# A two-layer hybrid backbone on one core: each engine's order set by a list scheduler in the kernel

## The chip, the cores and the metric

One Trainium2 chip, of which the program uses one core. A core has five engines that run at the same time, each through its own queue in order: TensorE (PE) multiplies matrices into PSUM, VectorE (DVE) and ScalarE (ACT) work on PSUM and SBUF, GpSimd (POOL) on SBUF, and SyncE (SP) issues most DMA transfers; GpSimd issues some too. They wait for each other by semaphores. The time is the device time of one execution, in microseconds (us); 1934.28 us is the median of three runs of the kernel before.

## The reference

Two layers over 512 latent tokens and 256 context tokens of 1024 channels, in float32. Each layer: a modulated norm, one input projection whose columns go to three head groups, an output projection with a gated residual, then a modulated norm, a SwiGLU feed-forward part and a gated residual:

```python
h_l = rmsnorm(x, norm1_g[i]) * (1.0 + sc1_l) + sh1_l
h_c = rmsnorm(ctx, norm1_g[i]) * (1.0 + sc1_c) + sh1_c
p_l = h_l @ w_in[i]
p_c = h_c @ w_in[i]
...
att_l = diff_attention(q_l, k_all, v_all, lam, subln_g[i], lam_init)
x = x + g1_l * mix_out(p_l, att_l, hy_params, sg_params, w_out[i])
x = x + g2_l * swiglu(rmsnorm(x, norm2_g[i]) * (1.0 + sc2_l) + sh2_l, ffn_w1[i], ffn_w2[i])
```

`mix_out` joins a Hyena group (two long convolutions, in the kernel by cosine and sine tables), a gMLP group (tokens mixed in chunks of 128) and differential attention (the difference of two softmaxes, with normalized and rotated queries and keys). The latent queries read context and latent keys, the context only itself; in the second layer the context is needed for its keys and values alone. The modulation values (shift, scale, gate) are a product of a conditioning vector with `ada_w`, six sections per layer.

## The kernel before

**Tiling.** Streams lie with channels on the partitions, eight tiles of 128 channels by 512 (latent) or 256 (context) tokens. Every operand of a large product is split into a high part (12 bits) and the exact rest, and `mm3` makes three multiplications of each pair: high by high (L251), high by low (L252), low by high (L253), 128x512 or 128x256 in size. A weight piece is fetched by SyncE into the arena FW, its high part is made by ScalarE (L232) and its low part by VectorE or GpSimd (L233) into the arena RW. R holds split operands, F float32 data, `banks` is PSUM (8 banks).

**Stages.** Four generators write the program: `lat_task` (the latent stream through both layers), `con_task` (the context stream), `side_task` (the filters' spectra, L902 and L903), `ada_task` (modulation, L401: 32 output columns a time, in four column groups of the array, eight instructions for a chunk of 256 channels; L375 turns the sums, L386 makes the gains G). `woven` takes the next step of whichever stream's matrix work is behind by hand-set rates (`CON`, `SIDE`, `ADA`, `WOVEN`). Memory is given out as the program is written: an arena's block or a PSUM bank goes to the next user when its owner's `free` has been called, so a later user waits for an earlier one on the chip.

**Order.** The instructions go to the framework in the order in which the generators write them. Its own scheduler then orders each engine's queue, by that order as priority and by its own durations, and adds the semaphores.

**Places that the prediction names.** `norm`: the squares are summed over channels (L279), a Newton iteration makes 1/rms (L261 to L267), TensorE spreads it over the partitions (L293), `modulate` scales and rounds on ScalarE (L503, L504), VectorE makes the low part (L507). `lambdas` and `rope_tables`: small constants, whose DMAs GpSimd issues and VectorE uses (L334, L354). `attend`: scores with 64 contracted rows, maximum (L683), factor (L686), exponentials on ScalarE (L688), the two softmaxes' difference (L692 to L694), transposes (L703), the product with the values. `sgu` is the gMLP group (L795 adds its bias). `fwd` of the Hyena group ends with rounding on ScalarE (L1036).

Of the kernel before, what the change touches and what calls it, by code (L numbers as in the profile page):

```python
# [9 lines left out]
F32 = mybir.dt.float32  # L10
# [6 lines left out]
P = 128  # L17
D = 1024
KT = D // P
SEQ = 512  # L20
# [18 lines left out]
class Buf:  # L39
    """A piece of an arena; emit-time lifetime, slices like a tile."""  # L40
# [11 lines left out]
class Arena:  # L52
    """Blocks of one tile, handed out longest-unused first, so that reuse waits little."""
# [40 lines left out]
    def fits(self, sizes):  # L94
        """Whether blocks of these units can be had, one beside the other."""
# [17 lines left out]
class Stream:  # L113
    """One token stream (latent or context) in channel-major form."""
# [10 lines left out]
# PSUM banks by use, arena sizes in KiB per partition.  # L125
BANKS = {"A": (0, 1, 6, 7), "S": (2, 3, 4, 5), "W": (6, 7), "P": (6, 7)}
UNITS = {"R": 104, "RW": 24, "F": 44, "FW": 24}
# Rates of the tasks in each phase (the latent stream has 10), and of the woven steps of each layer.
# [5 lines left out]
# Work of the latent and of the context stream that GpSimd does ("mix": 2 is all of it, 1 a half).  # L134
# [8 lines left out]
# Steps of the tasks that come first, the chunks of modulation weights that are fetched ahead, and  # L143
# the arenas of the weights of the first feed-forward tiles.
# [5 lines left out]
class Net:  # L150
# [16 lines left out]
    def woven(self, *tasks):  # L167
        """Generators (gen, rate) side by side; the matrix work of each grows at its rate.

        A rate may be a key of self.rates, which change with the phases."""  # L170
# [20 lines left out]
    def room(self, *sizes):  # L191
        """Waits until the float32 arena has room for the next step."""
        while not self.F.fits(sizes):
            yield "wait"

    def claim(self, n):
        """Waits until n units of the operand arena are spoken for by nobody."""
        while self.claimed + n > UNITS["R"]:
            yield "wait"
        self.claimed += n  # L200
# [22 lines left out]
    def tt(self, n, dtype=F32):  # L223
        """Tiny per-partition scratch, round robin."""
# [5 lines left out]
    def split(self, src, hi, lo, lo_eng=None):  # L230
        """hi = src rounded to 12 bits, lo = the rest, exactly."""
# [3 lines left out]
    def weights(self, src, *shape, pool=False, arena=None):  # L235
        """A split piece of weights of this shape; the low part by GpSimd if pool."""
# [8 lines left out]
    def mm3(self, out, terms):  # L245
        """out = sum of lhsT^T rhs over split terms: hi hi + hi lo + lo hi."""
# [9 lines left out]
    def rsqrt(self, ms, n, out=None):  # L256
        """1/sqrt by an exponent guess and three Newton steps."""
# [1362 lines left out]
```

## Time and profile before

| what | value |
|---|---|
| median of three runs | 1934.28 us (1927.73 to 1936.95) |
| span of the profiled execution | 1924.6 us |
| TensorE busy | 1813.6 us (94%) |
| VectorE busy | 1082.6 us (56%) |
| ScalarE busy | 689.1 us (36%) |
| GpSimd busy | 119.7 us (6%) |
| mean DMA rate | 128 GB/s |

The span runs from the first to the last instruction of one profiled execution; the timed runs are other executions, and their median lies 9.7 us above it. Matmuls are pipelined and a record's length contains the pipeline, so the pace of TensorE is read from start to start, not from the length of a record. The granted clock is the share of TensorE's full 2.4 GHz; 0.5 is its other level, 1.2 GHz, and a stretch between them is a mixture.

### The profile page before, as it was taken

To read this page: it belongs to the slowest core of one execution; us is meant where nothing else is said; L and a number is where in the kernel's file an instruction comes from. 1 tells how busy PE (TensorE), PEld (TensorE's weight loads), DVE (VectorE), ACT (ScalarE), POOL (GpSimd) and SP (SyncE) were. 2 spreads that over 40 slices of the span, in tenths; PEclk is the share of its full clock that TensorE was granted. 3 is DMA by queue.
4 is the path that set the end of the run, shared out by engine and by line. 5 is a ranking of instruction groups with operands and counts; after the bars stand their busy time and mean duration, and the time that the engine had idled before them with its cause. 6 is when DMAs were issued, how large, how long until landed. Compare 5 with 4: busy or idle time off the path is not lost.

```text
span 1924.6 us, 27933 instructions
## 1 busy us (share of the span) xinstructions
PE 1813.6 (94%) x11106; PEld 1558.6 (81%) x11106; DVE 1082.6 (56%) x2255; ACT 689.1 (36%) x1203; POOL 119.7 (6%) x128
## 2 busy tenths in 40 slices
PE   5799999789997999999999999899999999999999
PEld 2578898678776888888888888689988788888887
DVE  5677886778767523232423244789588773333333
ACT  2544434544544421212122112543455462222221
POOL 1100223211001000000000000011000000000000
PEclk9899899799997999999999999899999899999999
DMA  7567644235444343243424234444213222323231
GB/s 272 177 233 237 201 162 143 83 125 187 134 167 147 111 126 127 84 136 108 144 83 151 74 102 156 153 154 144 79 34 119 64 71 63 110 84 105 89 97 64
DMA packets 89564, 245.41 MB, mean 128 GB/s; under 512 B 9780, under 2 KB 21782, under 8 KB 89434
## 3 DMA queue, kind: packets, MB, share of 16 engines
q1 hardware_dynamic: 81162, 221.71, 35.2%
q0 software_dynamic: 8272, 21.92, 3.8%
q8 instruction: 87, 1.43, 0.3%
q14 instruction: 43, 0.35, 0.1%
HBM read 221.18 MB, written 22.41 MB: 127 GB/s over the span
## 4 chain that ended last, share of the span: by engine, by line
PE 79%; DVE 9%; DMA 4%; ACT 3%; issue 2%; POOL 0%; SPq 0%; ACTq 0%; DVEq 0%; POOLq 0%
PE banks L251 25%; PE banks L252 24%; PE banks L253 24%; PE banks L401 2%; PE banks L703 1%; DMA x_ctx<-F 1%; DVE RW L233 1%; DMA F<-x_ctx 1%; ACT F L688 1%; DVE tiny L683 1%; DVE F L1025 1%; PE banks L375 1%; PE banks L279 1%; DVE F L456 1%; DMA FW<-in_w_out 0%
## 5 line engine op out<-in xcount | busy, mean ns | idle before, releaser
L251 PE MATMUL banks<-R,RW 128*128 128x512 f32 (+1 forms) x1984 | 696.0, 352 | 9.1 <-ACT R L504 3.9
L252 PE MATMUL banks<-R,RW 128*128 128x512 f32 (+1 forms) x1984 | 693.9, 350 | 3.0 <-DVE R L507 3.0
L253 PE MATMUL banks<-R,RW 128*128 128x512 f32 (+1 forms) x1984 | 692.2, 349 | 0.5 <-DVE RW L233 0.5
L232 ACT ACTIVATE RW<-FW 128x1024 fp32r<-128x1024 f32 (+2 forms) x240 | 240.5, 1003 | 541.4 <-PE banks L252 418.9
L251 PEld LDWEIGHTS banks<-R,RW 128*128 128x128 f32 x1984 | 376.9, 190 | 64.7 <-ACT R L504 4.7
L252 PEld LDWEIGHTS banks<-R,RW 128*128 128x128 f32 x1984 | 377.0, 190 | 51.4 <-DVE R L507 3.8
L253 PEld LDWEIGHTS banks<-R,RW 128*128 128x128 f32 x1984 | 376.7, 190 | 50.4 <-issue 2.0
L233 DVE TENSOR_TENSOR RW<-FW,RW 128x1024 fp32r<-128x1024 f32 (+2 forms) x228 | 262.7, 1154 | 238.0 <-ACT RW L232 229.4
L1186 DVE SCALAR_TENSOR_TENSOR F<-banks,mods,F 128x512 f32<-128x512 f32 (+1 forms) x192 | 116.2, 615 | 177.4 <-PE banks L253 133.8
L251 PE MATMUL banks<-R 128*128 128x256 f32 (+3 forms) x584 | 188.0, 340 | 26.4 <-ACT R L1036 13.7
L252 PE MATMUL banks<-RW,R 128*128 128x256 f32 x624 | 180.0, 289 | 5.4 <-DVE RW L233 5.4
L251 PE MATMUL banks<-RW,R 128*128 128x256 f32 x624 | 181.1, 291 | 0.4 <-ACT F L552 0.2
L252 PE MATMUL banks<-R 128*128 128x256 f32 (+3 forms) x584 | 179.6, 319 | 1.4 <-DVE R L233 1.4
L253 PE MATMUL banks<-RW,R 128*128 128x256 f32 x624 | 180.2, 289 | 0.0
L253 PE MATMUL banks<-R 128*128 128x256 f32 (+3 forms) x584 | 177.5, 315 | 1.2 <-DVE R L1038 1.2
L251 PEld LDWEIGHTS banks<-R 128*128 128x128 f32 (+1 forms) x584 | 117.4, 209 | 49.6 <-ACT R L1036 15.2
L1204 DVE TENSOR_TENSOR F<-F,banks 128x256 f32<-128x256 f32 (+1 forms) x71 | 40.0, 565 | 208.5 <-PE banks L253 191.8
L232 ACT ACTIVATE R<-F 128x512 fp32r<-128x512 f32 (+1 forms) x133 | 72.0, 549 | 226.9 <-DVE F L1204 160.9
L252 PEld LDWEIGHTS banks<-R 128*128 128x128 f32 (+1 forms) x584 | 119.8, 209 | 10.0 <-issue 3.5
L252 PEld LDWEIGHTS banks<-RW,R 128*128 128x128 f32 x624 | 121.7, 195 | 7.6 <-DVE RW L233 6.3
L251 PEld LDWEIGHTS banks<-RW,R 128*128 128x128 f32 x624 | 121.5, 195 | 3.1 <-ACT F L552 0.8
L253 PEld LDWEIGHTS banks<-RW,R 128*128 128x128 f32 x624 | 121.8, 195 | 2.2 <-issue 1.5
(159 smaller groups left out, 1739.7 us busy)
## 6 DMA issues: line engine op xcount, KB each, us to landing
FW<-in_ffn_w SPq DMA_DIRECT2D x104, 512.0 KB, 3.7
FW<-in_ada_w SPq DMA_DIRECT2D x96, 512.0 KB, 5.0
FW<-in_w_in_tm SPq DMA_DIRECT2D x50, 512.0 KB, 4.8
R<-in_tab POOLq DMA_DIRECT2D x28, 512.0 KB, 4.9
FW<-in_w_in_cm SPq DMA_DIRECT2D x24, 512.0 KB, 4.7
F<-x_ctx SPq DMA_DIRECT2D x36, 256.0 KB, 3.6
FW<-in_ffn_w SPq DMA_DIRECT2D x24, 384.0 KB, 2.9
x_ctx<-F SPq DMA_DIRECT2D x32, 256.0 KB, 2.4
```

The costliest lines, as they stand in the source:

```text
L232: self.nc.scalar.activation(hi, src, AF.Copy)
L233: (lo_eng or self.nc.vector).tensor_tensor(lo, src, hi.bitcast(F32), op=ALU.subtract)
L251: mm(out, lhsT=lh, rhs=rh, start=(i == 0), stop=False)
L252: mm(out, lhsT=lh, rhs=rl, start=False, stop=False)
L253: mm(out, lhsT=ll, rhs=rh, start=False, stop=(i == n - 1))
L279: nc.tensor.matmul(p1[:, t:t + 1], lhsT=sq[:, t * P:(t + 1) * P], rhs=self.ones[:, 0:1], start=True, stop=True)
L375: nc.tensor.matmul(pt[:, b], lhsT=sb[:, b // 2, b % 2 * P:(b % 2 + 1) * P], rhs=self.pick, start=True, stop=True)
L401: nc.tensor.matmul(pa[32 * j:32 * j + 32, :], lhsT=self.cv[:, 4 * i + j, :], rhs=w[:, j, :], start=(i == 0), stop=(i == 1), tile_position= ...
L456: nc.vector.tensor_tensor(st.acc[:, cols], st.acc[:, cols], q.ap, op=ALU.add)
L683: nc.vector.tensor_reduce(m, b.ap, axis=AX.X, op=ALU.max)
L1186: self.nc.vector.scalar_tensor_tensor(x, p, self.mods[l][:, sec * 8 + k, st.v:st.v + 1], x, op0=ALU.mult, op1=ALU.add)
L1204: nc.vector.tensor_tensor(s.ap, s.ap, u, op=ALU.mult)
```

## The change

The generators, their rates and all arithmetic stay. What they call is no longer the framework but a recorder: `Plan.note` writes each instruction down with an engine, a duration (`took`), the time until its engine can take the next one (`pace`) and the pieces of memory that it writes and reads. At the end `needs` finds for each instruction those that it has to come after (values, and memory that is used again), `order` simulates the five engines and takes, whenever one is free, the ready instruction of the lowest rank, and `issue` hands the instructions to the framework in that order, with an edge from each to the next one on its engine, so that the framework's scheduler keeps it. The rank is three quarters the place in the old order and one quarter the length of the longest chain of work that hangs on the instruction. The rest of the diff deletes comments.

```diff
+class Plan:
...
+    def note(self, e, op, args, kw):
...
+        if op == "dma_start":
+            took, pace = math.prod(out.shape) * 4 / self.LINE, 50.0 if e == self.SP else 560.0
+        elif e == self.PE:
+            if op == "transpose":
+                pace, late, ins = 109.0, [args[1]], [args[2]]
+            else:
+                lhs, rhs = kw["lhsT"], kw["rhs"]
+                n, late, ins = size(rhs), [lhs], [rhs]
+                if rhs.dtype != F32 or lhs.dtype != F32:
+                    pace = max(n / self.RATE + 13.5, 109.0)
+                elif size(lhs) <= 32:
+                    pace = (2 * n / self.RATE + 6) / 4
+                else:
+                    pace = 2 * max(112.0, n / self.RATE)
+            took = pace + self.DRAIN
...
+    def order(self):
+        todo, needs = self.todo, self.needs()
+        n = len(todo)
+        rest, behind = [0.0] * n, [[] for _ in todo]
+        for k in range(n - 1, -1, -1):
+            rest[k] += todo[k][4] + (self.LANDING if todo[k][1] == "dma_start" else 0.0)
+            for j, kind in needs[k].items():
+                rest[j] = max(rest[j], rest[k])
+                behind[j].append((k, kind))
+        top = max(rest)
+        rank = [self.share * k / n - (1 - self.share) * rest[k] / top for k in range(n)]
...
+            now, e = best
+            while soon[e] and soon[e][0][0] <= now:
+                heapq.heappush(can[e], heapq.heappop(soon[e])[1:])
+            k = heapq.heappop(can[e])[1]
...
+    def issue(self):
+
+        nosync = mybir.DependencyInfo(mybir.DependencyClass.NoSync, mybir.DependencyReason.DATA)
+        last = [None] * 5
+        for k in self.order():
+            e, op, args, kw = self.todo[k][:4]
+            ins = getattr(getattr(self.tc.nc, Program.engines[e]), op)(*args, **kw).ins
+            if last[e] is not None:
+                self.tc.add_manual_dep(ins, last[e], nosync, reason="order")
+            last[e] = ins.name
+
+
 def network(ctx, tc, A):
+    tc = Plan(tc)
     net = Net(ctx, tc, A)
...
     run(woven((lat_gen, "lat"), (con_gen, "con"), (side, "side"),
               (ada, "ada")))
+    tc.issue()
```

What it does to the queues is seen at three places. A row is one instruction or, with x, several equal ones in a row; after the change all of them are created in `issue`, so that every row bears its line, L1561.

VectorE at the start of layer 0, before: the constants' steps (L334, `rope_...` of L354) among the low parts L507, 128x256 for the context, 128x512 for the latent stream.

```order
L386 SCALAR_TENSOR_TENSOR G_113<-mods_107,ng_111 128x16
L233 TENSOR_TENSOR RW<-FW,RW 128x1024
L334 TENSOR_TENSOR F<-F 128x256
L233 TENSOR_TENSOR RW<-FW,RW 128x1024
L507 TENSOR_TENSOR R<-F,R 128x256 x2
L336 TENSOR_REDUCE tiny<-F 128x4
L507 TENSOR_TENSOR R<-F,R 128x256
L932 SCALAR_TENSOR_TENSOR F<-banks,F 128x256
L936 SCALAR_TENSOR_TENSOR F<-banks,F 128x256
L507 TENSOR_TENSOR R<-F,R 128x256
L354 TENSOR_TENSOR rope_120<-F,qkg_119 128x512
L507 TENSOR_TENSOR R<-F,R 128x256 x2
```

The same place after the change; `F<-F 128x256` is L334, and one of the three in the third row is an L233 of the filters.

```order
L1561 SCALAR_TENSOR_TENSOR G_92<-mods_88,ng_91 128x16
L1561 TENSOR_TENSOR RW<-FW,RW 128x1024 x2
L1561 TENSOR_TENSOR R<-F,R 128x512 x3
L1561 TENSOR_TENSOR R<-F,R 128x256
L1561 TENSOR_TENSOR R<-F,R 128x512
L1561 TENSOR_TENSOR R<-F,R 128x256
L1561 TENSOR_TENSOR R<-F,R 128x512
L1561 TENSOR_TENSOR R<-F,R 128x256
L1561 TENSOR_TENSOR F<-F 128x256
L1561 TENSOR_REDUCE tiny<-F 128x4
```

Four latent L507 and three of the context have moved ahead of L334; before, all eight latent ones stood behind both constants.

TensorE near 605 us, before: L279 and L293 of the context's last norm in layer 0's mixer (`ones`, `ident,inv`) with the filters' L902 and L903.

```order
L252 MATMUL banks<-R 128x256
L253 MATMUL banks<-R 128x256
L279 MATMUL banks<-ones_104,F 128x1 x2
L903 MATMUL banks<-R 128x512
L902 MATMUL banks<-R 128x512
L279 MATMUL banks<-ones_104,F 128x1 x2
L903 MATMUL banks<-R 128x512
L293 MATMUL banks<-ident_100,inv 128x128 x4
L251 MATMUL banks<-R 128x256 x4
```

The same place after the change.

```order
L1561 MATMUL banks<-R 128x256 x18
L1561 MATMUL banks<-ones_87,F 128x1 x2
L1561 MATMUL banks<-R 128x512 x2
L1561 MATMUL banks<-ones_87,F 128x1 x2
L1561 MATMUL banks<-R 128x512 x6
L1561 MATMUL banks<-R 128x256 x25
L1561 MATMUL banks<-ident_85,inv 128x128 x4
L1561 MATMUL banks<-R 128x256 x10
```

Between the sums over channels (`ones`) and the spreading (`ident,inv`) there are now 31 multiplications, before there was one.

TensorE in the feed-forward part near 760 us, before: a chunk of modulation weights (`FW,cv`) between two sums.

```order
L252 MATMUL banks<-R,RW 128x256
L253 MATMUL banks<-R,RW 128x256
L401 MATMUL banks<-FW,cv_82 32x256 x8
L251 MATMUL banks<-R,RW 128x512
L252 MATMUL banks<-R,RW 128x512
```

The same place after the change.

```order
L1561 MATMUL banks<-R,RW 128x512 x6
L1561 MATMUL banks<-FW,cv_82 32x256
L1561 MATMUL banks<-R,RW 128x512
L1561 MATMUL banks<-FW,cv_82 32x256 x3
L1561 MATMUL banks<-R,RW 128x512
L1561 MATMUL banks<-FW,cv_82 32x256
L1561 MATMUL banks<-R,RW 128x512
L1561 MATMUL banks<-FW,cv_82 32x256 x3
L1561 MATMUL banks<-R,RW 128x512 x20
```

The run of eight has become four runs, with 128x512 multiplications between them.

## Rows read from the trace of the kernel before

**Rows 1.** The page: span, TensorE's busy time, the chain by engine.
```profile
span 1924.6 us, 27933 instructions
...
PE 1813.6 (94%) x11106; PEld 1558.6 (81%) x11106; DVE 1082.6 (56%) x2255; ACT 689.1 (36%) x1203; POOL 119.7 (6%) x128
...
PE 79%; DVE 9%; DMA 4%; ACT 3%; issue 2%; POOL 0%; SPq 0%; ACTq 0%; DVEq 0%; POOLq 0%
```

**Rows 2.** Busy time by stretch: length, engines (instructions), granted clock, DMA share, GB/s.
```profile
48.00:96.00 48.00, 35.80 (x149) 25.10 (x146) 30.02 (x70) 26.81 (x49) 5.52 (x6) 0.89 0.53 178
96.00:337.00 241.00, 229.17 (x1714) 204.12 (x1713) 185.26 (x446) 104.24 (x196) 47.75 (x51) 0.97 0.60 195
337.00:433.00 96.00, 79.12 (x495) 69.22 (x494) 74.88 (x169) 47.24 (x92) 21.54 (x16) 0.84 0.32 104
...
529.00:640.00 111.00, 98.81 (x658) 80.78 (x657) 79.60 (x198) 49.32 (x100) 9.97 (x12) 0.86 0.46 150
640.00:1200.00 560.00, 557.07 (x3375) 483.50 (x3374) 186.22 (x278) 123.37 (x190) 3.21 (x6) 1.00 0.36 117
...
1491.00:1587.00 96.00, 89.38 (x585) 80.88 (x584) 73.40 (x187) 52.57 (x105) 0.00 (x0) 0.91 0.22 68
```

**Rows 3.** The chain that ended last, from 47 us: start, length, what.
```profile
74.75 3.78 DMA F<-in_lam_p
...
79.27 5.60 DMA F<-in_rope
```

**Rows 4.** ScalarE in order of time, from 73 us: start, length, [idle before].
```profile
76.32 1.10 ACT L503 ACTIVATE F<-F,mods,G 128x256 f32<-128x256 f32 x2 [0.15 <-DVE G L386]
...
82.72 1.51 ACT L503 ACTIVATE F<-F,mods,G 128x512 f32<-128x512 f32 x2
```

**Rows 5.** TensorE in order of time, its waits from 47 to 90 us.
```profile
57.13 1.62 PE L902 MATMUL banks<-R 128*128 128x512 f32 x3 [3.24 <-DVE R L888]
...
80.16 0.38 PE L252 MATMUL banks<-RW,R 128*128 128x256 f32 x1 [2.00 <-DVE RW L233]
...
88.26 0.80 PE L252 MATMUL banks<-R,RW 128*128 128x512 f32 x1 [2.95 <-DVE R L507]
```

**Rows 6.** TensorE in order of time, three waits of the mixer.
```profile
229.64 0.65 PE L293 MATMUL banks<-ident,inv 128*128 128x128 f32 x4 [1.87 <-DVE inv L267]
...
346.39 0.33 PE L251 MATMUL banks<-R 128*128 128x128 f32 x1 [3.90 <-ACT R L1036]
...
605.47 1.09 PE L293 MATMUL banks<-ident,inv 128*128 128x128 f32 x4 [4.12 <-DVE inv L267]
```

**Rows 7.** TensorE in order of time, a wait of the Hyena group.
```profile
295.22 0.39 PE L251 MATMUL banks<-R 128*128 128x256 f32 x1 [2.67 <-ACT R L1036]
```

**Rows 8.** TensorE in order of time around modulation multiplications (L401).
```profile
647.20 0.62 PE L401 MATMUL banks<-FW,cv 128*32 128x256 f32 x2
647.74 0.39 PE L252 MATMUL banks<-R,RW 128*128 128x256 f32 x1
647.97 0.28 PE L253 MATMUL banks<-R,RW 128*128 128x256 f32 x1
648.09 0.28 PE L251 MATMUL banks<-R,RW 128*128 128x256 f32 x1
...
648.33 0.28 PE L253 MATMUL banks<-R,RW 128*128 128x256 f32 x1
648.53 0.63 PE L401 MATMUL banks<-FW,cv 128*32 128x256 f32 x6
649.10 0.38 PE L251 MATMUL banks<-R,RW 128*128 128x256 f32 x1
...
687.28 1.07 PE L401 MATMUL banks<-FW,cv 128*32 128x256 f32 x16
688.28 1.05 PE L375 MATMUL banks<-pick,F 128*128 128x2 f32 x8
```

**Rows 9.** VectorE in order of time, a wait at 360 us.
```profile
360.73 0.42 DVE L795 TENSOR_TENSOR F<-banks,F 64x256 f32<-64x256 f32 x1 [3.23 <-ACT RW L232]
```

157 lines of the change are left out of this document (added).

## Prediction

> **What bounds the kernel now.** I read the page first, then the busy time by stretch, then TensorE in order of time where it stops. TensorE is busy for 1813.6 us of a span of 1924.6 us and holds 79% of the chain that ended last [rows 1], so the kernel can lose at most the 111 us in which TensorE stands still, plus what is hidden inside its busy time: multiplications at half clock and changes of its mode. The reader is to see in [rows 2] where these lie. From 640 to 1200 us, the feed-forward part, TensorE is busy 557.07 of 560 us at a granted clock of 1.00: a better order has nothing to fill there and can only do harm. The idle time is in the mixers: 12.2 us in 48 to 96, 11.8 us in 96 to 337, 16.9 us in 337 to 433, 12.2 us in 529 to 640, 6.6 us in 1491 to 1587. In the same five stretches the granted clock is 0.89, 0.97, 0.84, 0.86 and 0.91; one minus that, times the length, is 5.3 + 7.2 + 15.4 + 15.5 + 8.6 = 52 us of clock not granted. VectorE is busy three quarters of 337 to 433 and of 1491 to 1587 (74.88 and 73.40 of 96 us), so TensorE is not alone in setting the pace there.
>
> **What the change is, part by part.** The same 14560 instructions stand in the program, and the memory and PSUM places are given out as before; each engine's order is new, and pinned. Median shifts are small: 6 places on TensorE, 1 on VectorE and ScalarE, 0 on the two DMA queues (GpSimd, SyncE). So no stage changes; what changes is which work stands under a wait. All sums are against the profiled span of 1924.6 us; the median of the runs, 1934.28 us, is 9.7 us above it, and I take that difference as unchanged.
>
> **Start of layer 0 (gain).** After 74.75 us the chain runs through two constants: VectorE stands at L334 until `in_lam_p` has landed (3.78 us) and at L354 until `in_rope` has (5.60 us) [rows 3]. Behind them in its queue wait the subtractions of L507, which make the low parts of the normalized streams, and TensorE waits for these: 2.00 us at 80.16, 2.95 us at 88.26 [rows 5]. ScalarE takes the context's eight channel tiles first, from 76.32, and the latent's only from 82.72 us [rows 4]. In the new order four latent L507 stand ahead of L334 and seven ahead of the first L354, latent and context tiles alternate, and 16 modulation multiplications come forward under TensorE's wait of 3.24 us at 57.13 [rows 5]; with them the gain G, which ScalarE waits for at 76.32, can be ready earlier. The three waits sum to 8.2 us, and ScalarE's work of some 16 us (76.32 to about 92.6) is as long as before: what is won is its earlier start. **-8 us**; the bounds are 0 (G comes no earlier, since ScalarE's queue holds the copies of G's sums behind others) and the stretch's whole 12.2 us.
>
> **Waits with work put under them (gain), and the ones it is taken from (loss).** At 346.39 TensorE stands 3.90 us for ScalarE's L1036 [rows 6]. In the new order 33 more multiplications of 128x256 stand ahead of it; at 0.12 us each (648.09 less 647.97 [rows 8]) that is 3.96 us, enough. In the old order these 33 run from about 355 us on, and the sums that VectorE's L795 reads stand behind them: VectorE idles 3.23 us before it, at 360.73 [rows 9] (the row names ScalarE's L232; what L795 reads is written by TensorE just before). One move serves both. At 605.47 TensorE stands 4.12 us for the last Newton step L267 [rows 6]; 25 multiplications, 3.0 us, and five of the filters' 128x512 come ahead of it, so all of it goes. At 229.64 (1.87 us [rows 6]) 20 or more come ahead, 2.4 us. Together 9.9 us. Against that, at 295.22 the order takes some 2.3 us of work away from ahead of a wait of 2.67 us [rows 7], and a twin of it near 328 us loses as much. **-6 us**, bounds -10 and +5: the work pulled forward is the reserve of a later wait.
>
> **Other waits in the mixers (gain).** Of the idle 16.9 + 12.2 + 6.6 us in 337 to 433, 529 to 640 and 1491 to 1587 [rows 2], 8 us are the two waits above. The other 27.7 us are many waits of about 1 us on the softmax's VectorE steps. There the new order keeps a chain's steps together (L692, L693, L694 follow each other) and puts big, patient subtractions behind. I take a third, **-9 us**; bounds 0, if VectorE, three quarters busy, is itself the limit, and -18.
>
> **Half-clock stretches (gain).** The rows show the granted clock low in stretches where TensorE stood still. If a quarter of the idle time goes, part of the 52 us comes back; a tenth is **-5 us**, bounds 0 and -15. The Trainium skill, "TensorE: Matmul & The Clock Gate", section "What's actually happening", calls the throttled state the default that activity releases; by that rule filled waits pay twice, which is rival B below, and the trace agrees so far that the busiest stretch has 1.00.
>
> **Modulation multiplications pulled apart (loss).** These (L401) have 32 output columns, four side by side. Eight in one run, 16 records, take 1.00 us from 687.28 to 688.28; one alone, two records, holds TensorE from 647.20 to 647.74, 0.54 us, and a run of three 0.57 us (648.53 to 649.10) [rows 8]. So any run up to four costs about 0.55 us, and entering one costs 0.20 us instead of 0.12 (648.33 to 648.53). Before there are 53 runs, 43 of them of eight; the new order has 95: 61 of one to four (32 of a single one), 33 of six to eight, one of 16. In 640 to 1200 us three groups of eight become four runs each: 3 x (4 x 0.64 - 1.09) = 4.4 us; three more and one at 636 us leave a single one behind: 4 x 0.65 = 2.6 us. TensorE is never idle there, so these 7 us are all on the path. Before 636 us ten groups are cut, one of them into eight singles (8 x 0.64 - 1.09 = 4.0 us): 15.7 us in all by the same prices, and I count half, 8 us, since TensorE idles by turns there. **+15 us**, bounds 7 and 23. The planner gives such a multiplication a fixed 55 ns wherever it stands, so nothing in it works against this. The Trainium skill, "TensorEngine Tiling (Array Packing)", section "Key Properties", says that a change of the tiling mode drains TensorE and that tiles of one mode run in parallel; it speaks against this change and names no price, and [rows 8] agree. By the rule alone the 42 more runs would be a loss of unknown size; by the rows they are 7 to 23 us.
>
> **At nothing.** In the feed-forward part sums of two or three PSUM banks now alternate, multiplication by multiplication; 128x256 and 128x512 follow each other at their own pace either way, and the cover is TensorE itself. If the later end of a sum held back the weights' next piece, the 2.9 us of idle there would grow. The 64-row score multiplications change row half more often (60 neighbours instead of 32) and meet 128-row ones more often (28 more): the one helps and the other hurts, 28 times each; I count zero, and 28 x 0.1 = 3 us either way, by what entering L401 costs. On SyncE and GpSimd's queue hardly a transfer moves.
>
> **The sum.** -8 - 6 - 9 - 5 + 15 = -13 us, and small waits under 1 us, which I have not listed, should give some more: I take -5 for them. That is -18 us: a span of about 1907 and a time of **1916 us**.
>
> **Rivals.**
> A, the sum as it stands: 1916 us, 0.9% faster.
> B, the waits fall by half and the clock holds: of 111 us idle 40 go, 15 of the clock come back, 15 are lost to L401: 1934 - 40 = 1894 us. For it: idle and low clock lie in the same stretches [rows 2], and at 346 one move served two engines. Against it: VectorE's share there.
> C, the waits only move. What is pulled under one wait is missed at the next, as at 295.22 [rows 7]; the start's 8 us and a few others are paid back by L401: 1931 us, no change.
> D, slower: L401's mode changes all lie on the path. Place: the ten groups before 636 us and the seven from there on; price 23 us, from [rows 8]. It decides the sign once the filled waits bring less than 13 us in all. With the start alone (-8) the time is 1934 + 23 - 8 = 1949 us. For it: TensorE is busy 229 of 241 us in 96 to 337, where six of the groups lie [rows 2].
> That the change does not do what it says can be left out: its order differs from the old one on all five engines.
>
> **How the numbers follow.** A 0.42, B 0.17, C 0.23, D 0.18. A runs from 1905 to 1924, B down to 1880, C from 1925 to 1943, D up to 1960. Leaving out the lower half of B and most of D beyond 1945 leaves 1885 to 1945 us for 8 in 10. This kernel's runs differ by 0.5% (1927.73 to 1936.95), so 0.5%, 1924.6 to 1944.0 us, is about what can be told from no change. A and B make faster 0.59, C 0.23, D 0.18.
>
> **What would show it.** Right: the first latent L507 of layer 0 before 80 us, no DMA of `in_lam_p` or `in_rope` on the chain, no TensorE wait over 1 us near 346 and 605 us, idle time of TensorE at some 85 us instead of 111, granted clock above 0.9 in 337 to 433 and 529 to 640. L401 would show runs of 0.55 us where eight took 1.00, and 640 to 1200 us would be some 7 us longer. Wrong: TensorE's idle time unchanged, with new waits where work was taken away (near 295 and 328 us); or split L401 runs that cost less than 0.55 us because other multiplications run beside them.

## The result and the profile after

The changed kernel takes 1959.66 us (median of four runs, 1955.32 to 1962.23) against 1935.62 us before: a ratio of 1.014 with an interval of 1.0104 to 1.0175. It is 1.4% slower, outside the range and on the other side than forecast. The profiled span grew by 32.5 us, more than the 24.0 us between the medians: the profiled execution of before lies 11.0 us under its median, that of the change 2.6 us under its own.

The page of the changed kernel, its span, busy times and chain, beside [rows 1]:

```profile
span 1957.1 us, 27967 instructions
...
PE 1859.6 (95%) x11106; PEld 1565.7 (80%) x11106; DVE 1077.7 (55%) x2255; ACT 687.5 (35%) x1202; POOL 116.6 (6%) x128
...
PE 84%; DVE 8%; ACT 3%; DMA 2%; issue 2%; POOL 0%; SPq 0%; DVEq 0%; ACTq 0%; POOLq 0%
```

TensorE stands still 13.5 us less (97.5 instead of 111.0 us), and yet the time is longer: it is busy 46 us more with the same multiplications. The order fills gaps, but here it also changed what the busy engine's work costs. The busy time by stretch, beside [rows 2]:

```profile
48.00:96.00 48.00, 43.97 (x254) 33.00 (x243) 38.10 (x83) 31.73 (x57) 5.51 (x6) 0.89 0.45 141
96.00:337.00 241.00, 223.09 (x1511) 187.09 (x1510) 167.98 (x405) 91.85 (x175) 41.10 (x47) 0.93 0.58 184
337.00:433.00 96.00, 82.55 (x500) 69.39 (x498) 71.32 (x169) 45.94 (x94) 24.43 (x19) 0.82 0.29 92
433.00:529.00 96.00, 89.02 (x620) 77.67 (x620) 68.80 (x173) 42.69 (x81) 8.24 (x5) 0.91 0.53 159
529.00:640.00 111.00, 102.88 (x600) 78.31 (x599) 73.38 (x175) 47.77 (x97) 6.18 (x8) 0.88 0.42 131
640.00:1200.00 560.00, 559.85 (x3385) 476.00 (x3384) 190.36 (x307) 123.42 (x196) 4.48 (x5) 1.00 0.36 114
```

The first row has 254 multiplications instead of 149: the start is ahead. In the second there are 203 fewer (1511, 1714 before) in the same 241 us: the lead is gone before 337 us.

To see what the busy time holds, I took both traces apart in the same way: from the start of each multiplication to the start of the next, less the pace at full clock (0.227 us for 512 columns, 0.120 us for 256; 1.1 us for a run of eight L401, which are the 32-column modulation multiplications). What is left is first standing still (the next starts after the record's end), then half clock (half the time worked in stretches at the lower level), and the rest is put to the neighbours' shapes:

| where TensorE's time goes beyond its pace, us | before | after | difference |
|---|---|---|---|
| ahead of the first multiplication | 6.9 | 3.1 | -3.8 |
| standing still | 99.6 | 90.0 | -9.6 |
| half clock | 47.2 | 61.9 | +14.7 |
| next to an L401 | 12.9 | 37.8 | +24.9 |
| next to a 64-row score | 13.3 | 22.9 | +9.6 |
| all else | 40.2 | 37.2 | -3.0 |

They sum to +32.8 us, the 32.5 of the span within rounding. One limit of the table lies in the first 100 us. The record of the granted clock begins at 73.6 us in the trace of before and at 51.0 us in that of the change, and the profile counts full clock ahead of it. Before, these sixteen records of L401 took twice the 1.07 us of [rows 8]:

```profile
21.64 2.24 PE L401 MATMUL banks<-FW,cv 128*32 128x256 f32 x16 [11.81 <-DMA FW<-in_ada_w]
```

So the half clock of the start stands under "next to an L401" and "all else" in both columns (9 to 10 us next to L401 in each), and the 0.89 for 48 to 96 us in [rows 2] is too high: another trace of the old order (the pinned run below), whose record begins at 31.4 us, shows 0.68.

```profile
48.00:96.00 48.00, 35.59 (x158) 24.20 (x151) 30.54 (x71) 27.00 (x49) 5.53 (x6) 0.68 0.54 181
```

From the work of 105 us on, where every record is complete, half clock is 42.7 us before, 42.1 in the pinned run and 56.8 after the change; next to L401 it is 1.5, 1.5 and 27.9 us. Both rows of the table hold.

The table's differences by stretch, where equal work ends a stretch in both traces (times of before): to 105 us -17, 105 to 200 +16, 200 to 240 +11, 240 to 433 +2, 433 to 529 +10.5, 529 to 640 0, 640 to 1200 +6, 1200 to 1300 -5, 1300 to 1587 +9.5.

**L401.** TensorE of the changed kernel in order of time, where a chunk of eight is cut into eight:

```profile
156.77 0.28 PE L1561 MATMUL banks<-RW,R 128*128 128x256 f32 x1
156.98 0.62 PE L1561 MATMUL banks<-FW,cv 128*32 128x256 f32 x2
157.53 0.38 PE L1561 MATMUL banks<-R 128*128 128x256 f32 x1
157.84 0.62 PE L1561 MATMUL banks<-FW,cv 128*32 128x256 f32 x2
158.39 0.39 PE L1561 MATMUL banks<-RW,R 128*128 128x256 f32 x1
158.71 0.62 PE L1561 MATMUL banks<-FW,cv 128*32 128x256 f32 x2
```

A single one takes 0.55 us (156.98 to 157.53), and the 128x256 behind it 0.31 us (157.53 to 157.84) instead of its 0.12: 0.74 us in all for one of eight multiplications that took 1.00 us together in one run [rows 8].

**Scores.** The same engine, where single 64-row multiplications of two scores stand between 128x512 ones:

```profile
137.70 0.49 PE L1561 MATMUL banks<-R,RW 128*128 128x512 f32 x1
138.13 0.38 PE L1561 MATMUL banks<-R 64*128 64x256 f32 x1
138.44 0.50 PE L1561 MATMUL banks<-R,RW 128*128 128x512 f32 x1
138.87 1.48 PE L1561 MATMUL banks<-R 64*128 64x256 f32 x7
```

The 64-row one takes 0.31 us (138.13 to 138.44), the 128x512 one 0.43 us (137.70 to 138.13, and 138.44 to 138.87) instead of 0.227. The last row groups neighbours of two shapes under the first one's. This pair loses 0.39 us (0.31 + 0.43 - 0.227 - 0.12), and it comes again and again from 136 to 144.5 us.

**Waits.** Waits that the prediction followed, after the change:

```profile
246.73 0.65 PE L1561 MATMUL banks<-ident,inv 128*128 128x128 f32 x4 [1.01 <-DVE inv L1561]
...
304.85 1.23 PE L1561 MATMUL banks<-R 128*128 128x256 f32 x4 [4.12 <-ACT R L1561]
...
359.58 0.66 PE L1561 MATMUL banks<-R 128*128 128x128 f32 x4 [2.90 <-ACT R L1561]
361.31 1.05 PE L1561 MATMUL banks<-R 128*128 128x128 f32 x5 [1.07 <-ACT R L1561]
...
631.99 0.60 PE L1561 MATMUL banks<-ident,inv 128*128 128x128 f32 x4
```

The last one, 4.12 us at 605.47 in [rows 6], is gone, as is the twin near 328 us (1.42 us), against the forecast; the first has gone from 1.87 to 1.01 us. The one at 346.39 is there in two pieces (2.90 + 1.07 us for 3.90), in spite of the 33 multiplications ahead of it, and that of [rows 7] grew from 2.67 to 4.12 us.

**A queue that stands behind one step.** The largest new loss of the mixers lies near 205 us. ScalarE in order of time, then VectorE, then TensorE, all of the changed kernel:

```profile
204.64 1.06 ACT L1561 ACTIVATE RW<-FW 128x1024 fp32r<-128x1024 f32 x1 [8.97 <-issue]
205.60 0.40 ACT L1561 ACTIVATE R<-F 128x256 fp32r<-128x256 f32 x1
```

```profile
205.73 1.23 DVE L1561 TENSOR_TENSOR RW<-FW,RW 128x1024 fp32r<-128x1024 f32 x1 [9.08 <-ACT RW L1561]
206.87 0.41 DVE L1561 TENSOR_TENSOR R<-F,R 64x256 fp32r<-64x256 f32 x1
```

```profile
193.38 11.17 PE L1561 MATMUL banks<-RW,R 128*128 128x256 f32 x91
204.39 0.27 PE L1561 MATMUL banks<-ident,F 128*128 128x128 f32 x1
206.05 0.73 PE L1561 MATMUL banks<-R 128*128 128x512 f32 x2 [1.39 <-ACT R L1561]
207.33 0.73 PE L1561 MATMUL banks<-R 64*128 64x512 f32 x2 [0.55 <-DVE R L1561]
208.61 1.93 PE L1561 MATMUL banks<-R 64*128 64x256 f32 x6 [0.55 <-DVE F L1561]
211.96 1.01 PE L1561 MATMUL banks<-R 64*128 64x256 f32 x3 [1.42 <-ACT F L1561]
215.78 1.80 PE L1561 MATMUL banks<-R 64*128 64x256 f32 x4 [2.82 <-ACT F L1561]
```

ScalarE stands 8.97 us at the high part of a weight piece (`RW<-FW`, L232 before). The profile puts it down to nothing it shows ("issue"); by the kernel's use of memory the piece overwrites a place of RW that the 91 multiplications read, and it starts as the last of them has ended (193.38 + 11.17 = 204.55 us). Behind it waits a small step of the filters (`R<-F` 128x256, L884), and for that one TensorE's L902 at 206.05. Filters and scores share four PSUM banks (`BANKS["S"]`), so the scores follow only at 208.61, with the softmax's waits and nothing left to put under them, since the 91 multiplications are done. Before, the scores ran among the piece's multiplications: at 197.63, with 65 of them still to come.

### The profile page after: what moved, and what is told of

Read it like the earlier page. It is cut to its first block, busy times and chain, and to the rows that moved or that the text cites. A ratio compares the mean times of both kernels' runs of the same rounds, so it can differ in the third digit from the quotient of the medians.

```text
span 1957.1 us, 27967 instructions
## 1 busy us (share of the span) xinstructions
PE 1859.6 (95%) x11106; PEld 1565.7 (80%) x11106; DVE 1077.7 (55%) x2255; ACT 687.5 (35%) x1202; POOL 116.6 (6%) x128
## 3 DMA queue, kind: packets, MB, share of 16 engines
q1 hardware_dynamic: 81162, 221.71, 35.4%
## 4 chain that ended last, share of the span: by engine, by line
PE 84%; DVE 8%; ACT 3%; DMA 2%; issue 2%; POOL 0%; SPq 0%; DVEq 0%; ACTq 0%; POOLq 0%
PE banks L1561 84%; DVE F L1561 5%; DMA FW<-in_ada_w 1%; ACT F L1561 1%; DVE tiny L1561 1%; DVE R L1561 1%; DVE RW L1561 1%; ACT R L1561 1%; ACT RW L1561 0%; DMA F<-in_hy_w 0%; DMA x_ctx<-F 0%; POOL F L1561 0%; DMA F<-kd 0%; DMA F<-x_ctx 0%; SPq L1561 0%
## 5 line engine op out<-in xcount | busy, mean ns | idle before, releaser
L1561 PE MATMUL banks<-R,RW 128*128 128x512 f32 (+1 forms) x5952 | 1177.1, 353 | 8.3 <-ACT R L1561 4.0
L1561 PEld LDWEIGHTS banks<-R,RW 128*128 128x128 f32 x5952 | 965.2, 190 | 179.9 <-issue 23.1
L1561 ACT ACTIVATE RW<-FW 128x1024 fp32r<-128x1024 f32 (+2 forms) x240 | 240.0, 1002 | 616.4 <-PE banks L1561 533.4
L1561 DVE TENSOR_TENSOR RW<-FW,RW 128x1024 fp32r<-128x1024 f32 (+2 forms) x228 | 264.9, 1164 | 285.9 <-ACT RW L1561 273.0
L1561 PE MATMUL banks<-R 128*128 128x256 f32 (+4 forms) x1792 | 341.4, 336 | 34.8 <-ACT R L1561 16.6
L1561 PEld LDWEIGHTS banks<-R 128*128 128x128 f32 (+1 forms) x1792 | 271.9, 212 | 84.9 <-issue 22.0
L1561 PE MATMUL banks<-RW,R 128*128 128x256 f32 x1872 | 264.7, 289 | 4.3 <-DVE RW L1561 3.9
L1561 PEld LDWEIGHTS banks<-RW,R 128*128 128x128 f32 x1872 | 243.0, 193 | 16.8 <-issue 6.6
L1561 ACT ACTIVATE F<-banks 128x256 f32<-128x256 f32 (+1 forms) x232 | 106.4, 475 | 290.9 <-PE banks L1561 256.1
L1561 DVE TENSOR_TENSOR F<-F,banks 128x256 f32<-128x256 f32 (+1 forms) x169 | 81.7, 509 | 217.3 <-PE banks L1561 197.3
L1561 DVE SCALAR_TENSOR_TENSOR F<-banks,mods,F 128x512 f32<-128x512 f32 (+1 forms) x192 | 115.4, 614 | 154.6 <-PE banks L1561 152.5
L1561 ACT ACTIVATE R<-F 128x512 fp32r<-128x512 f32 (+2 forms) x235 | 120.3, 526 | 151.2 <-DVE F L1561 123.0
L1561 DVE TENSOR_TENSOR R<-F,R 128x512 fp32r<-128x512 f32 (+2 forms) x227 | 126.9, 572 | 40.0 <-ACT R L1561 39.1
L1561 DVE TENSOR_TENSOR F<-F 128x256 f32<-128x256 f32 (+1 forms) x188 | 116.1, 637 | 11.7 <-ACT F L1561 7.3
L1561 ACT ACTIVATE F<-banks,tiny,rq 128x768 f32<-128x768 f32 (+1 forms) x80 | 72.2, 904 | 53.5 <-DVE tiny L1561 44.3
L1561 PE MATMUL banks<-FW,cv 128*32 128x256 f32 x768 | 82.5, 428 | 1.5 <-DMA FW<-in_ada_w 1.1
L1561 DVE TENSOR_REDUCE tiny<-banks 128x1 f32<-128x768 f32 (+1 forms) x80 | 67.1, 845 | 28.3 <-PE banks L1561 27.8
L1561 PE MATMUL banks<-ident,F 128*128 128x128 f32 x336 | 66.5, 310 | 15.7 <-DVE F L1561 8.5
L1561 ACT ACTIVATE R<-banks 128x512 fp32r<-128x512 f32 (+1 forms) x114 | 54.0, 509 | 72.5 <-PE banks L1561 72.3
L1561 DVE TENSOR_TENSOR R<-banks,R 128x512 fp32r<-128x512 f32 (+1 forms) x114 | 63.3, 576 | 16.1 <-ACT R L1561 16.0
L1561 PEld LDWEIGHTS banks<-ident,F 128*128 128x128 f32 x336 | 44.9, 157 | 28.9 <-DVE F L1561 11.4
L1561 POOL TENSOR_TENSOR F<-F 128x256 f32<-128x256 f32 (+1 forms) x40 | 46.4, 1163 | 210.0 <-DVE F L1561 125.9
```

Source lines behind the costliest of these rows:

```text
L1561: ins = getattr(getattr(self.tc.nc, Program.engines[e]), op)(*args, **kw).ins
```

## The experiments

All ratios are to the kernel before, run beside them on the same chip (its median was 1929.6 to 1933.8 us there, 1935.62 beside the change). Where a text below says how much a run is "less than the change", it compares medians of different chips; by the ratios, L401 whole is worth 15 us, scores whole alone 11 and the rate alone 13, each within some 9 us by the two intervals. "Whole" edits are made in `order`, where the planner picks:

```diff
         todo, needs = self.todo, self.needs()
         n = len(todo)
+        head = list(range(n))
+        for k in range(1, n):
+            if self.mode(k) and self.mode(k) == self.mode(k - 1) and k - head[k - 1] < 8:
+                head[k] = head[k - 1]
+                needs[k].setdefault(head[k], 1)
...
         rank = [self.share * k / n - (1 - self.share) * rest[k] / top for k in range(n)]
+        rank = [x if head[k] == k else -10.0 for k, x in enumerate(rank)]
```

`mode` names a float32 multiplication of 32 columns (L401), a rounded one of 64 rows (a score), or both: once the first of a group is issued, the rest come next.

**L401 whole** (`mode` names L401 alone).

> The changed kernel, with the eight modulation multiplications (L401) of a chunk kept together (49 runs instead of 95). Theory: the extra time is mode changes on TensorE's path. In the traces, the time of TensorE beyond its pace in intervals that touch L401 grew from 12.9 to 37.8 us; with whole chunks some 24 us come back: 1933 to 1940 us. Rival: the cuts filled slots in which TensorE would have stood still, and the loss is moved waits (as the 8 us near 210 us): idle time grows by what the cuts free, and the time stays at 1952 us or above.

Measured: 1939.83 us, ratio 1.0062 (1.0038 to 1.0086), 19.8 us less than the change, at the upper end of the theory. The time next to L401 is 9.6 us instead of 37.8 (what is left is the start), standing still 94.7 instead of 90.0. The rival falls: the cuts were on the path, some 5 us of them in time that TensorE now stands.

**Scores whole as well.**

> As e1_ada_whole, and the scores' 64-row multiplications of a block (three or six) kept together too: 67 runs of them instead of 105. Theory: intervals that touch 64-row multiplications cost 13.3 us beyond the pace before and 22.9 after; about 10 us less than e1_ada_whole, 1924 to 1931 us. Rival: the alternation with 128-row multiplications stood under the wait for the softmax anyway: within 3 us of e1_ada_whole. On the clock: if half speed (47 us lost before, 62 after) follows the standing still of TensorE, e1 and e2 keep 55 to 65 us of it; if it follows the cut modes, it falls below 50 us.

Measured: 1922.3 us, 0.9957 (0.9934 to 0.9981), 1.7 us below the expected range; the rival, within 3 us of the run ahead, falls. The time next to 64-row multiplications falls from 23.6 to 15.4 us, and half clock stays at 61.9 (62.2 in the run with L401 whole alone). So half clock hangs on neither kind of cut, as the expectation had it for a loss that follows waits.

**Scores whole alone**, L401 still cut.

> The changed kernel with the scores' 64-row multiplications kept together (67 runs of them instead of 105) and L401 as cut as in the changed kernel (99 runs). Between e1_ada_whole and e2_ada_scores_whole the medians fell by 17.5 us, the profiled spans by 11.0. Theory: the scores' price is that of the mode changes alone, some 8 to 10 us by the trace: 1947 to 1953 us. Rival: earlier scores also shorten the softmax's waits, 17 us: 1939 to 1945 us.

Measured: 1950.9 us, 1.0083 (1.0053 to 1.0112), 8.8 us less than the change. The 17.5 us between the two medians above are no more than the mode changes and the scatter of these runs; the profiled spans there differed by 11.0.

**The old order, pinned.** `order` returns the kernel before's sequence, written out as a table.

> The new way of issuing with the old order: the queue of each engine is that of the kernel before, pinned by the same edges. Theory: pinning and recording cost nothing, only the order does: 1931 to 1939 us. Rival: the edges or other semaphores cost something by themselves: 1945 us or more.

Measured: 1929.52 us, 1.0009 (0.9989 to 1.0029). Writing down and pinning cost nothing that can be seen (0.3% at most); the order alone does.

**No pull of the longest chain.**

```diff
-    def __init__(self, tc, share=0.75):
+    def __init__(self, tc, share=1.0):
```

> The changed kernel with a rank that is the place in the old writing order alone (share 1.0 instead of 0.75), no pull of the longest chain. L401 falls to 50 runs, the 64-row scores to 74. Theory: the quarter of the rank that pulls long chains makes the cuts; without it both prices go as in e2_ada_scores_whole, 1924 to 1935 us, if the start's gain (some 16 us at 100 us) stays. Rival: the start's gain comes from that quarter too and goes with it: 1940 to 1948 us.

Measured: 1933.01 us, 1.0025 (1.001 to 1.004). The cuts go (1.0 us next to L401, 13.6 next to the scores), as does a part of the start's gain (13 us ahead at 105 us instead of 17). Half clock is as in the change (56.2 us from 105 us on, 56.8 there), standing still is 76.8 us there instead of 69.4, and 337 to 433 us takes 8.7 us longer than before. The pull of the longest chain is what cut the runs; it was also worth something elsewhere. The time lies in the theory's range, near its upper end.

**The cut alone**, in the old order: 14 runs of L401 cut into eight.

> The price of a cut by itself: the order of the kernel before on all engines, but 14 runs of eight modulation multiplications between 640 and 1200 us are cut into eight single ones with a 128x256 multiplication between each two (98 more runs, nothing else moves). By the prediction's price (0.64 us a single, 1.09 a run of eight) each costs 4.0 us, 56 us in all: 1988 us. By the rows of the changed kernel (a single 0.55 us, and 0.31 instead of 0.12 us for the multiplication behind it) 4.7 us, 66 us in all: 1998 us. Rival: the single ones run beside the 128x256 multiplications and cost under 2 us each: below 1960 us.

Measured: 2001.79 us, 1.0369 (1.0308 to 1.0431); 68.0 us for 14 cuts, 4.9 us each. TensorE in order of time, at one of them:

```profile
1061.90 0.62 PE L1492 MATMUL banks<-FW,cv 128*32 128x256 f32 x2
1062.45 0.39 PE L1492 MATMUL banks<-R,RW 128*128 128x256 f32 x1
1062.77 0.62 PE L1492 MATMUL banks<-FW,cv 128*32 128x256 f32 x2
```

0.55 us, then 0.32 us (1062.45 to 1062.77), the clock at 1.00. Each further run costs 0.69 us (68.0 us for 98; by the rows 8 x 0.74 less 1.19 us for the whole run, over seven, 0.68). The Trainium skill, "TensorEngine Tiling (Array Packing)", section "Key Properties", says that changing the tiling mode drains TensorE; this run agrees so far that each change has a price.

**The planner's transfer rate.** One number, `LINE` in `Plan`, from 230.0 to 340.0 (GB/s), on top of both "whole" edits.

> As e2_ada_scores_whole, with one number of the planner changed: its transfer rate 340 instead of 230 GB/s. In the changed kernel ScalarE stands 9.0 us at 204.64 and VectorE 9.1 us at 205.73: the next weight piece's high part, which has to wait until 91 multiplications have read the old piece, is put ahead of a small step of the filters, whose data the planner expected 13 us after their issue; the transfers move 340 to 420 GB/s there. Theory: an error of the planner's clock sets a patient step ahead of a ready one; with the faster rate the order turns round, TensorE's idle time and half clock near 200 to 230 us (10 and 10 us in e2, 3 and 3 before) go back: 1908 to 1914 us. Rival: with another rate other steps stand in each other's way; 1918 us or more.

Measured: 1910.78 us, 0.9883 (0.9862 to 0.9903). ScalarE and TensorE of this run at the same work:

```profile
187.96 0.42 ACT L1578 ACTIVATE R<-F 128x256 fp32r<-128x256 f32 x1 [5.25 <-DMA F<-hid]
```

```profile
188.43 1.39 PE L1578 MATMUL banks<-R 128*128 128x512 f32 x4 [2.35 <-ACT R L1578]
189.75 1.04 PE L1578 MATMUL banks<-RW,R 128*128 128x256 f32 x6
190.72 1.01 PE L1578 MATMUL banks<-R 64*128 64x256 f32 x3
191.66 1.22 PE L1578 MATMUL banks<-RW,R 128*128 128x256 f32 x4
192.81 1.01 PE L1578 MATMUL banks<-R 64*128 64x256 f32 x3
193.75 3.75 PE L1578 MATMUL banks<-RW,R 128*128 128x256 f32 x16
```

The small step now stands ahead and waits for its own transfer alone; the scores run among the multiplications of the weight piece again, and after one wait of 2.35 us TensorE does not stop. The granted clock shows the rest. The stretch of equal work in four kernels (length, busy times, granted clock): before, the change, both kinds whole, and with the faster rate:

```profile
200.00:240.00 40.00, 36.71 (x267) 33.52 (x266) 35.42 (x99) 20.83 (x43) 10.58 (x12) 0.92 0.67 212
```

```profile
199.00:250.00 51.00, 41.44 (x264) 34.87 (x263) 38.89 (x107) 23.16 (x46) 12.93 (x13) 0.80 0.53 175
```

```profile
187.00:241.00 54.00, 44.54 (x264) 37.84 (x263) 39.01 (x106) 23.24 (x46) 14.07 (x13) 0.75 0.51 166
```

```profile
195.00:233.00 38.00, 34.96 (x270) 32.00 (x270) 35.34 (x102) 19.29 (x40) 12.41 (x12) 0.97 0.69 222
```

Some 265 multiplications take 40, 51, 54 and 38 us. TensorE's idle time in them is 3.3, 9.6, 9.5 and 3.0 us, and where it is larger the granted clock is lower: 0.92, 0.80, 0.75, 0.97. The second price of a wait is here as large as the first: in the third kernel standing still and half clock cost 9.5 and 10.1 us, in the fourth 3.0 and 1.1. The Trainium skill, "TensorE: Matmul & The Clock Gate", section "What's actually happening", calls the throttled state the default that activity releases; these four rows agree. Rival B's sentence, that filled waits pay twice, holds in this stretch in the other direction: new waits cost twice.

**The rate alone**, on the changed kernel.

> The changed kernel with the transfer rate 340 instead of 230 GB/s and nothing else: L401 stays cut (101 runs), the 64-row scores too (104). Theory: the three causes add up, and this one is worth some 11 us as between e2 and e6: 1945 to 1951 us. Rival: the wrong rate was also what pulled the modulation and the scores apart; below 1935 us.

Measured: 1947.81 us, 1.0075 (1.0044 to 1.0107), 11.9 us less than the change. The time lies in the theory's range, and L401 is as cut as ever, so the rate is not what cut the runs. The three causes taken singly are worth 19.8, 8.8 and 11.9 us, 40.5 in all; taken together, 1959.66 - 1910.78 = 48.9 us. From the work of 105 us on, the traces show what each edit takes away, in us:

| kernel | standing still | half clock | next to L401 |
|---|---|---|---|
| before | 71.5 | 42.7 | 1.5 |
| old order, pinned | 72.1 | 42.1 | 1.5 |
| the change | 69.4 | 56.8 | 27.9 |
| L401 whole | 73.9 | 56.2 | 0.0 |
| both kinds whole | 68.0 | 58.8 | 0.0 |
| rate alone | 61.1 | 43.7 | 31.8 |
| both kinds whole and rate | 70.6 | 35.4 | -0.2 |

Half clock falls with the rate, by 13 us on the changed kernel and by 23 us on the one with whole runs, and with no other edit; it does not follow the total of standing still. All five traces of planned orders with the old rate have 56 to 59 us of it, the three with the faster rate 35 to 44. A trace of the old order scatters less than that: 42 to 43 us in three, 51 in the run with the cut alone.

**A right price for L401 in the planner**, on top of the faster rate: `pace = 150.0` instead of `(2 * n / self.RATE + 6) / 4`.

> As e6_dma_rate_340, and the planner prices a modulation multiplication at 150 ns instead of 55 (eight then take 1.2 us, what a whole run and its entry take in the traces). Theory: with the runs kept whole the planner's error of some 0.7 us in each of 48 places shifts its clock, but the order near each wait is set by the rank: within 5 us of e6. Rival: its clock decides which step is put ahead, as at 204 us: more than 5 us away from e6.

Measured: 1915.43 us, 0.9904 (0.9882 to 0.9926), 4.7 us above. Within the 5 us of the theory, though not by much: a truer price that the rank does not use shows no gain here.

**The start alone**: the first 524 instructions in the order of the run with both kinds whole, all others in the old order.

> The 524 instructions that e2_ada_scores_whole has begun by its 88th us, in its order; all others in the order of the kernel before. Theory: the start is a gain by itself, 12 to 13 us, and the old order keeps it: 1914 to 1919 us. Rival: the lead is only work pulled forward; the old order meets the same supply of data some 20 us later, and 6 us or less are left: 1922 to 1930 us.

Measured: 1912.22 us, 0.9894 (0.9869 to 0.9919). The start is worth 16.5 us by the spans (1924.6 to 1908.1; 20.2 by the medians beside each other), more than either expectation, and the old order keeps all of it. What the change lost behind 105 us was not owed by the start.

**The best order of each stretch**, from the traces of before and of both kinds whole.

> By stretches the order that lost less: e2's up to 105 us (of the old time), the old one to 337, e2's to 433, the old one to 580, e2's to 1491, the old one to the end. Theory: gains and losses of the stretches are local and add up: 12 + 6 + 6 us below the kernel before, 1903 to 1909 us. Rival: what one stretch gains the next one pays: 1915 us or more.

Measured: 1895.23 us, 0.9803 (0.978 to 0.9827), the fastest of all, 8 us better than the expected range and some 2% faster than the kernel before. Its page:

```profile
span 1894.1 us, 27949 instructions
...
PE 1803.1 (95%) x11106; PEld 1549.6 (82%) x11106; DVE 1079.5 (57%) x2255; ACT 686.1 (36%) x1202; POOL 118.5 (6%) x128
```

Standing still is 83.3 us (99.6 before), half clock 40.0 (47.2).

**The same with stretches of the two faster-rate kernels.**

> As e8_best_stretches, with the stretch from 337 to 433 us in the order of e6_dma_rate_340 (9.2 us below the old one there, e2 in e8 4.4), 529 to 640 in that of e9_ada_price (7.0 below, e8 3.6), the old order from 1300 us on. If gains of stretches add up: some 8 us below e8's 1895, 1885 to 1890 us. Rival: a stretch's gain hangs on how the stretch ahead of it ended; 1895 us or more.

Measured: 1905.08 us, 0.9883 (0.9813 to 0.9954). The expectation fails, and by the trace mostly at one place: 337 to 433 us, 9.2 us shorter than before in the kernel that it is taken from, takes 0.6 us longer here, with 14.1 us of standing still (12.0 there) and 14.9 of half clock (5.7 there). That fits the rival, that a stretch hangs on how the one ahead of it ended, but it is not shown: the clock alone scatters as much. In traces of the unchanged old order the same stretch has 12.3, 12.2 and 14.9 us of half clock (before, pinned, start alone), and 1300 to 1491 us has 1.6, 1.5 and 9.6 (before, pinned, the cut alone).

## Why the prediction was wrong

**Which steps failed.** Two steps came out with the wrong sign: "other waits" (-14 us with the small ones) and "half clock" (-5 us), forecast at -19 us together and measured at about +18. A third, put at nothing, cost about 9 us: the 64-row scores. L401 was right in its mechanism and 5 us short in size; the start was right, and its gain twice the forecast. What the runs showed behind the first two is an error that the sum had no term for, the planner's transfer rate: alone it is worth 11.9 us and gives back 13 of the 14 us of half clock.

| step of the sum | forecast, us | measured, us | from |
|---|---|---|---|
| start of layer 0 | -8 | -16.5 | start alone, spans |
| three filled waits and two robbed ones | -6 | -4.9 | their rows: 14.0 to 9.1 |
| other waits | -14 (-9 and -5) | +3 | standing still, less these five and the start's 7.6 |
| half clock | -5 | +14.7 | the two traces |
| L401 | +15 | +19.8 (15 by the ratios) | L401 whole |
| 64-row scores | 0, 3 either way | +8.8 (11 by the ratios) | scores whole alone |

The measured terms come from different runs and overlap; that they sum to +24.9 us, near the 24.0 between the medians, is in part chance.

**Start: right, forecast at half its size.** VectorE of the changed kernel, from the first latent L507 to L334 (70.59 us):

```profile
64.14 0.68 DVE L1561 TENSOR_TENSOR R<-F,R 128x512 fp32r<-128x512 f32 x1
65.07 1.63 DVE L1561 TENSOR_TENSOR R<-F,R 128x512 fp32r<-128x512 f32 x3 [0.25 <-ACT R L1561]
67.62 1.03 DVE L1561 TENSOR_TENSOR R<-F,R 128x512 fp32r<-128x512 f32 x2 [0.92 <-ACT R L1561]
69.64 1.03 DVE L1561 TENSOR_TENSOR R<-F,R 128x512 fp32r<-128x512 f32 x2 [1.00 <-ACT R L1561]
70.59 0.42 DVE L1561 TENSOR_TENSOR F<-F 128x256 f32<-128x256 f32 x1
```

Four of the 128x512 in the first four rows are latent ones (the fifth is an L233), and the context's lie inside the groups. Four latent ones stand ahead of L334, as the order says, and the first comes by 66 us, where before ScalarE had its latent tiles only from 82.72 us [rows 4]. Neither `in_lam_p` nor `in_rope` is on the chain up to 110 us. The sum took the three waits for the whole gain, but the first multiplication also starts 3.8 us earlier, and the work after the waits is denser.

**L401: the mechanism was right, the term mis-sized, in two ways.** The price of a run left out its exit, which stood in [rows 8]: behind an L401 the 128x256 takes 0.23 us (647.74 to 647.97), 0.11 more than its pace, besides the 0.08 us ahead of it. With it a single costs 0.55 + 0.08 + 0.11 = 0.74 us and a run of eight cut into eight 4.7 us, not 4.0. And half of the ten groups before 636 us was written off because TensorE idles there by turns. It does, but not where these groups stand: next to L401 the time up to 640 us grew by 17.5 us, against 8 forecast. From 640 to 1200 us it grew by 7.4, against 7.0. Six of the groups lie in 96 to 337 us; from 96 to 200 us alone the change loses 8.8 us next to L401, while TensorE is busy 100.7 of 104 us. What is on the path is decided by the place, not by the mean of all stretches.

**64-row scores: the step "at nothing" failed.** It took the price from entering L401, where 128-row multiplications surround it, and set 28 gains against 28 losses. The entries were counted, but not what a single one between two 128-row ones costs both ways: 0.39 us. By that price 28 more cost 11 us; the measured 9 to 10 us leave little that standing side by side can have given back.

**Half clock: the wrong sign.** The step took the clock as a share of the idle time: less idle, more clock. The total of standing still did fall, and half clock rose by 14 us all the same; the total does not set it. At 200 to 240 us the place is seen: TensorE stands 0.55 to 2.82 us five times from 204 to 216 us in the changed kernel, and half clock in this work is 2.9 us before, 6.6 after, 1.4 with the rate alone. That waits close together are what costs the clock elsewhere too was not tried. The prediction's 52 us of clock not granted also took 0.89 for 48 to 96 us, which the record's late begin makes too high.

**Other waits: the planner's clock was not looked into.** The prediction took it that a chain's steps kept together would shorten the mixers' waits, and it gave rival C, that waits only move, 0.23. At 200 to 240 us they moved because the planner expected a transfer late: 13 us from issue to end by its own durations, as the expectation of that run has it, for what the chip did in under 7 (issued at 181.31, used at 187.96 in the run with the faster rate). The rate stood in the code and the rates of the transfers in the trace. The wrong duration did not only misplace a step here; in a pinned order it stopped a whole queue behind it.

**Rival D had a mechanism that proved true, and its time was partly luck.** Its 23 us lie near the 19.8 measured, and it was given 0.18 because the halved price was believed. But the start's 16.5 us nearly pay for the cuts, and its condition, that the filled waits bring less than 13 us in all, failed at the start alone; the sign was decided by the scores, the moved waits and the clock, which D did not have. Rival C named the moved waits, as a tie. The measured 1959.66 us lies at D's upper end, 1960, because these losses came on top of a start twice as good.

**The signs.** Of those named for being right, the early latent L507, the chain, the 0.55 us runs of L401 and the 6 us more in 640 to 1200 us came true. TensorE's idle time (97.5 us, not some 85), the granted clock (0.82 and 0.88, not above 0.9) and the wait near 346 us did not.

## What to carry to other kernels

A list scheduler that knows durations but not what two neighbours on an engine cost each other can scatter work that is cheap only in a row; give such groups one place in the order, and compare the busy time, not only the idle time, of the two orders. A pinned order can turn an error of the planner's clock into a queue that stands behind a step that is not ready, so measure its transfer times before its finer points: here the rate was worth 11.9 us and a truer price of L401 nothing. Look where the clock's record begins before you compare clocks. Keeping the better order of each stretch worked once (1895 us); a second choice of stretches, expected better still, took 1905 us.

## What was not expected of the hardware

A 64-row multiplication alone between 128x512 ones takes 0.31 us and its neighbour 0.43 us instead of 0.227. A run of one 32-column multiplication holds TensorE for 0.54 us and a run of three for 0.57 us [rows 8], and a single one costs the next 128x256 another 0.19 us where a second such one follows. Both prices showed at full clock. One number of the planner moved the time lost at half clock by 13 and 23 us, while the total of standing still fell by 8 us and rose by 3. From 190 to 201 us of the changed kernel the transfers moved 102 to 428 GB/s in slices of half a microsecond, over half of the slices above 300, with a mean of 125 over its span.
